# Neighbour sums on one core: 8 of 32 destination blocks from gathered rows, 24 dense, and X split by accumulating DMA

## The chip, the cores and the metric

The kernel runs on one core of one Trainium2 chip. Its time is the device time of one execution in microseconds; the kernel before takes 510.82 us as the median of 3 runs (510.23 to 510.98). TensorE (PE) multiplies matrices and loads weights (PEld), VectorE (DVE) and ScalarE (ACT) work along rows of 128 partitions, GpSimd (POOL) and SyncE (SP) mainly issue DMAs here. Each engine works through its own instructions in order and waits on semaphores of the others.

## The reference

```python
num_nodes, num_edges, dim = 4096, 65536, 128
output = np.zeros((num_nodes, dim), dtype=np.float32)
for i in range(len(edge_index_src)):
    output[edge_index_dst[i]] += node_features[edge_index_src[i]]
```

Source and destination indices are drawn at random, so that each of the 1024 pairs of a destination block and a source block (128 nodes each, 32 blocks) holds some 64 edges. Features are float32, and the sum must come out at float32 precision.

## The kernel before

The kernel turns the sum into dense matrix products. For a destination block d and a source block s, a 128 by 128 matrix A counts the edges from each source node to each destination node, and the output block is the sum over s of A transposed times the rows of X of block s. X is held as three bf16 parts whose sum is the float32 value (`x3`), so each product is made three times and summed in PSUM.

To build A, the edges have to be brought together by pair (d, s). The 65,536 edges lie as 128 partitions times 512, and are looked at as NCH = 24 chunks of up to NJ = 22 edges per partition. Two passes sort them:

- **Pass 1** (lines 105 to 195) sorts each chunk by destination block. A one-hot over the 32 blocks (`oh1`, line 128) is summed over the edges with a matmul against a triangle (`before`, line 131) and a chain of 21 adds (`cum1`, line 152), which gives each edge its rank in its block (`rank1`, lines 157 to 165). Then, for six quads of four chunks, a one-hot of the rank (`p1`, line 176 in the helper `onehot`) is multiplied against the keys (`v1`, line 141): 88 or 84 matmuls a quad (line 190). The results `sa` and `sbk` (lines 194 and 195) hold, for each chunk and block, up to 128 edges along the partitions.
- **The split of X** (lines 198 to 204) loads four quarters on the SP queue and makes the three bf16 parts by copies on ACT and subtractions on DVE in turn.
- **Pass 2** (`pass2`, lines 210 to 264) does the same again for a group of GD = 8 destination blocks, by source block: one-hots (line 215), counts (219), 23 adds (228), a product with the one-hot (229), ranks (232, 236), and for each destination block a one-hot of 24 by 128 (`p2`, line 176) and 24 matmuls (251). It is a generator; the main loop takes one step of it per slot.
- **The main loop** (lines 305 to 325) has a slot for each of the 32 destination blocks. `onehots` (line 276) builds two one-hots of 32 by 128 on DVE, `blocks` multiplies them into A for eight source blocks at a time (line 286, evicted by ACT at line 288), and `product` multiplies A of the slot before with `x3` (line 293: 96 matmuls of 128 by 128). `finish` copies the result on ACT (line 298) and stores it.

The order is written out by hand (`manual_schedule`): every engine runs its instructions in the order of the Python code. A pool with two buffers (`sb2`) lets DVE be up to two slots ahead of PE. `_general` is a slow path for inputs whose counts do not fit; it is behind a flag and does not run here.

Of the kernel before, what the change touches and what calls it, by code (L numbers as in the profile page):

```python
# [8 lines left out]
P = 128  # L9
# [7 lines left out]
NB = 32  # L17
NCH = 24
NJ = 22
NQ = NCH // 4  # L20
GD = 8
CODE0 = 0x2000


@with_exitstack
def kernel(
# [14 lines left out]

    nc = tc.nc
# [7 lines left out]
    flagp = ctx.enter_context(tc.tile_pool(name="flagp", bufs=1))  # L50
    fmax = flagp.tile([P, 8], F32, name="fmax")
    flag_i = flagp.tile([1, 1], I32, name="flag_i")

# [3 lines left out]
    with ExitStack() as fast:  # L57
        fast.enter_context(tc.manual_schedule())
        _fast(fast, tc, node_features, src32, dst32, out, cst, ident, fmax, flag_i, T)
# [6 lines left out]
def _fast(ctx, tc, X, src32, dst32, out, cst, ident, fmax, flag_i, T):  # L66
    nc = tc.nc
    V, S, G, PE = nc.vector, nc.scalar, nc.gpsimd, nc.tensor

    sb1 = ctx.enter_context(tc.tile_pool(name="sb1", bufs=1))  # L70
    sb2 = ctx.enter_context(tc.tile_pool(name="sb2", bufs=2))
    ps = ctx.enter_context(tc.tile_pool(name="ps", bufs=2, space=bass.MemoryType.PSUM))
# [3 lines left out]
    raw = sb1.tile([P, 7 * NT], I32, name="raw", tag="cum")  # L76
# [8 lines left out]
    V.memset(raws[:, T:, :], 0)  # L85

    identb = cst.tile([P, P], BF16, name="identb")
    V.tensor_copy(out=identb[:], in_=ident[:])

    before = cst.tile([P, P], BF16, name="before")  # L90
    G.memset(before[:], 1.0)
    G.affine_select(out=before[:], in_=before[:], pattern=[[1, P]], base=0,
                    channel_multiplier=-1, compare_op=OP.is_gt, fill=0.0)
    iota = cst.tile([P, P], U16, name="iota")
    G.iota(iota[:], pattern=[[1, P]], base=0, channel_multiplier=0)

    x3 = cst.tile([P, NB, 3, P], BF16, name="x3")
# [4 lines left out]
    kd = sb1.tile([P, NCH * NJ], BF16, name="kd")  # L102
# [3 lines left out]
    V.tensor_copy(out=kd[:], in_=blk_i)  # L106
# [5 lines left out]

    def by_quad(t):
        return t.rearrange("p (j q l) -> p q j l", q=NQ, l=4)

    S.activation(out=kb[:], in_=by_quad(sblk_i), func=mybir.ActivationFunctionType.Copy, bias=1.0)
    S.activation(out=ka[:], in_=by_quad(code_i), func=mybir.ActivationFunctionType.Copy,
                 bias=float(CODE0))
# [3 lines left out]

    JQ = NJ * NQ
    oh1 = sb1.tile([P, JQ, NB, 4], BF16, name="oh1", tag="oh")
    kdv = kd[:].rearrange("p (m l) -> p m l", l=4)
    psb = [ps.tile([P, 1024], F32, name=f"psb{h}", tag="psA") for h in range(2)]
    for b in range(NB):
        V.tensor_single_scalar(out=oh1[:, :, b, :], in_=kdv, scalar=float(b), op=OP.is_equal)
    for h in range(2):
        for j in range(NJ):  # L130
            PE.matmul(out=psb[h][:, :384], lhsT=before[:],  # L131
                      rhs=oh1[:, j * NQ:(j + 1) * NQ, 16 * h:16 * h + 16, :],
                      start=j == 0, stop=j == NJ - 1)
# [3 lines left out]
    def spread1(q):  # L137
        v1[q] = sb2.tile([P, NJ, 2, NB, 4], BF16, name="v1", tag="t1")
        ohq = oh1[:].rearrange("p (j q) b l -> p q j b l", q=NQ)[:, q]
        for k, key in ((0, kab), (1, kb[:])):  # L140
            V.tensor_tensor(out=v1[q][:, :, k], in0=ohq,  # L141
                            in1=key[:, q, :, None, :].to_broadcast([P, NJ, NB, 4]), op=OP.mult)

    spread1(0)
    cum1 = sb1.tile([P, NJ, NQ, NB, 4], BF16, name="cum1", tag="cum")
    oh1j = oh1[:].rearrange("p (j q) b l -> p j (q b l)", q=NQ)
    cum1j = cum1[:].rearrange("p j q b l -> p j (q b l)")
    for h in range(2):
        S.copy(out=cum1[:, 0, :, 16 * h:16 * h + 16, :],
               in_=psb[h][:, :384].rearrange("p (q b l) -> p q b l", q=NQ, b=16))  # L150
    for j in range(1, NJ):
        V.tensor_tensor(out=cum1j[:, j], in0=cum1j[:, j - 1], in1=oh1j[:, j - 1], op=OP.add)  # L152
    HJ = NJ // 2
    rank1 = sb1.tile([P, NQ, NJ, 4, 2], BF16, name="rank1")
    for h in range(2):
        js = slice(h * HJ, (h + 1) * HJ)
        V.tensor_tensor(out=cum1j[:, js], in0=cum1j[:, js], in1=oh1j[:, js], op=OP.mult)  # L157
        psr = ps.tile([P, 512], F32, name="psr", tag="misc")
        for b in range(NB):
            PE.matmul(out=psr[:, :HJ * NCH], lhsT=identb[:],  # L160
                      rhs=cum1[:, js, :, b, :].rearrange("p j q l -> p (j q) l"),
                      start=b == 0, stop=b == NB - 1)
        for k in range(2):
            S.copy(out=rank1[:, :, js, :, k],
                   in_=psr[:, :HJ * NCH].rearrange("p (j q l) -> p q j l", q=NQ, l=4))
    spread1(1)
    V.tensor_reduce(out=fmax[:, 0:1], in_=rank1[:].rearrange("p q j l k -> p (q j l k)"),
                    op=OP.max, axis=AX.X)


# [3 lines left out]
    def onehot(dst, keys2, n):  # L174

        V.tensor_tensor(  # L176
            out=dst.rearrange("p i (m k) -> p i m k", k=2),
            in0=iota[:, None, :].to_broadcast([P, n, P]).rearrange("p i (m k) -> p i m k", k=2),
            in1=keys2[:, :, None, :].to_broadcast([P, n, P // 2, 2]), op=OP.is_equal)

    for q in range(NQ):
        if q > 1:
            spread1(q)
        p1 = sb2.tile([P, NJ * 4, P], BF16, name="p1", tag="t2")
        onehot(p1[:], rank1[:, q].rearrange("p j l k -> p (j l) k"), NJ * 4)
        psm = ps.tile([P, 512], F32, name="psm", tag="misc")
        for l in range(4):
            js = [j for j in range(NJ) if j * NCH + q * 4 + l < T]
            for j in js:
                PE.matmul(out=psm[:, l * 64:(l + 1) * 64], lhsT=p1[:, j * 4 + l, :],  # L190
                          rhs=v1[q][:, j, :, :, l].rearrange("p k b -> p (k b)"),
                          start=j == js[0], stop=j == js[-1])
        pv = psm[:, :256].rearrange("p (l k b) -> p l k b", l=4, k=2)
        S.copy(out=sa[:, q * 4:q * 4 + 4, :], in_=pv[:, :, 0, :])
        S.copy(out=sbk[:, q * 4:q * 4 + 4, :], in_=pv[:, :, 1, :])


    for i in range(0, NB, 8):
        xf = sb2.tile([P, 8, P], F32, name="xf")
        nc.sync.dma_start(out=xf[:], in_=X[i * P:(i + 8) * P, :].rearrange("(s p) f -> p s f", p=P))  # L200
        for v in range(3):
            S.copy(out=x3[:, i:i + 8, v, :], in_=xf[:])  # L202
            if v < 2:
                V.tensor_tensor(out=xf[:], in0=xf[:], in1=x3[:, i:i + 8, v, :], op=OP.subtract)  # L204
# [3 lines left out]
    state = {}  # L208

    def pass2(g):  # L210
        d0 = g * GD
# [33 lines left out]
        for half in range(2):  # L245
# [9 lines left out]
            if half == 0:  # L255
                yield
# [166 lines left out]
```

## Time and profile before

| | |
|---|---|
| time, median of 3 runs | 510.82 us |
| the profiled execution's own time | 509.85 us |
| its span, first to last instruction | 507.9 us |
| mean granted TensorE clock | 0.818 |
| PE busy | 375.5 us (74%) |
| DVE busy | 366.0 us (72%) |
| ACT busy | 163.1 us (32%) |
| POOL busy | 1.5 us |
| DMA, all queues | 6.05 MB, mean 12 GB/s |

The span is the time from the first to the last instruction of the profiled execution; the execution took 1.95 us more than it, and the median of the runs is another 0.97 us longer. The busy shares of PE and DVE are near each other, but they are averages over stages in which now one and now the other is the bound, so the stages have to be read apart. The rows that the working rests on are quoted in the prediction. In them, L131 is line 131 of the kernel, "x44" a count of instructions, "busy, mean ns" the sum in us and the mean of one in ns, and what stands after the second bar is the idle time before them and what ended it.

### The profile page before, as it was taken

The page shows a single profiled execution, that of the slowest core. Times are in us where ns is not written, and L with a number is a line of the kernel's source. Part 1 is how long each engine was busy: PE and PEld are TensorE (multiplying, and loading weights), DVE is VectorE, ACT ScalarE, POOL GpSimd, SP SyncE. Part 2 cuts the span into 40 slices and gives each one's busy share as a digit, 9 for nine tenths or more (in the row PEclk, how much of TensorE's full clock was granted, in tenths as well). Part 3 has the DMA queues.
Part 4 walks back from the last instruction along what each step waited for, and adds up shares of the span by engine and source line. Part 5 has one row for each costly group of instructions (what it writes and reads, how often), then busy time and mean ns, then how long its engine had stood idle before and what let it go on. Part 6 is the DMA issues. An engine that isn't in the chain of part 4 may idle for free.

```text
span 507.9 us, 12335 instructions
## 1 busy us (share of the span) xinstructions
PE 375.5 (74%) x5709; PEld 358.5 (71%) x5709; DVE 366.0 (72%) x429; ACT 163.1 (32%) x213; POOL 1.5 (0%) x10
## 2 busy tenths in 40 slices
PE   0607574610339283999999499999949999999997
PEld 0305574610238283999999499999949999999996
DVE  5697999735859899566789956678995666655630
ACT  1001000045000050332656133265613326665652
POOL 1000000000000000000000000000000000000000
PEclk9957766665665596987999798799979879999999
DMA  5000000011000000000000000000000000000000
GB/s 165 1 0 1 1 1 0 1 43 41 0 0 1 2 1 5 8 6 3 12 14 8 5 8 6 3 12 13 8 5 8 7 2 13 13 9 12 12 13 14
DMA packets 9109, 6.05 MB, mean 12 GB/s; under 512 B 608, under 2 KB 8800, under 8 KB 9056
## 3 DMA queue, kind: packets, MB, share of 16 engines
q1 hardware_dynamic: 8912, 4.72, 3.3%
q8 instruction: 45, 0.74, 0.6%
q10 hardware_dynamic: 144, 0.52, 0.3%
q14 instruction: 8, 0.07, 0.0%
HBM read 3.15 MB, written 2.10 MB: 10 GB/s over the span
## 4 chain that ended last, share of the span: by engine, by line
PE 59%; DVE 31%; issue 5%; ACT 3%; DMA 1%; DVEq 0%; ACTq 0%
PE pso L293 32%; PE psa L286 11%; DVE p L176 9%; DVE cum L228 5%; PE ps L251 5%; PE psr L232 4%; DVE oh L276 4%; PE psb L219 3%; DVE cum L229 3%; DVE v L141 2%; DVE cum L152 2%; ACT x L202 2%; DVE xf L204 2%; PE psr L160 2%; PE psb L131 2%
## 5 line engine op out<-in xcount | busy, mean ns | idle before, releaser
L293 PE MATMUL pso<-x,a 128*128 128x128 bf16 x3072 | 200.2, 224 | 0.0
L293 PEld LDWEIGHTS <-a 128*128 128x128 bf16 x3072 | 185.3, 100 | 0.0
L288 ACT CAST a<-psa 128x1024 bf16<-128x1024 f32 x128 | 129.2, 1013 | 87.3 <-PE psa L286 87.0
L176 DVE TENSOR_TENSOR p<-iota,rank 128x3072 bf16<-128x3072 uint16 (+1 forms) x38 | 90.8, 2426 | 24.3 <-PE ps L251 24.3
L276 DVE TENSOR_TENSOR oh<-iotas,slo 128x4096 bf16<-128x4096 uint16 x32 | 73.2, 2289 | 45.1 <-PE psa L286 45.1
L286 PE MATMUL psa<-oh 128*128 128x128 bf16 x1024 | 81.8, 226 | 1.3 <-ACT a L288 1.3
L276 DVE TENSOR_TENSOR oh<-iota,dlo 128x4096 bf16<-128x4096 uint16 x32 | 73.1, 2284 | 0.0
L286 PEld LDWEIGHTS <-oh 128*128 128x128 bf16 x1024 | 65.9, 101 | 1.7 <-issue 1.6
L251 PE MATMUL ps<-ov,p 128*128 128x32 bf16 x768 | 50.2, 238 | 6.7 <-DVE p L176 6.0
L251 PEld LDWEIGHTS <-p 128*128 128x128 bf16 x768 | 46.1, 120 | 10.2 <-DVE p L176 10.2
L190 PE MATMUL psm<-v,p 128*128 128x64 bf16 x512 | 31.7, 239 | 23.6 <-DVE p L176 23.1
L190 PEld LDWEIGHTS <-p 128*128 128x128 bf16 x512 | 30.6, 123 | 24.7 <-DVE p L176 24.7
L232 PE MATMUL psr<-cum,identb 128*128 128x192 bf16 x128 | 20.2, 354 | 32.8 <-DVE cum L229 32.8
L232 PEld LDWEIGHTS <-identb 128*128 128x128 bf16 x128 | 18.3, 144 | 34.7 <-issue 21.8
L219 PE MATMUL psb<-ov,before 128*128 128x256 bf16 x96 | 14.5, 322 | 35.2 <-DVE ov L215 35.2
L219 PEld LDWEIGHTS <-before 128*128 128x128 bf16 x96 | 10.9, 115 | 38.2 <-issue 26.0
L228 DVE TENSOR_TENSOR cum<-cum,ov 128x256 bf16<-128x256 bf16 x92 | 26.8, 291 | 4.4 <-ACT cum L222 1.4
L160 PE MATMUL psr<-cum,identb 128*128 128x264 bf16 x64 | 9.7, 323 | 17.5 <-DVE cum L157 17.5
L204 DVE TENSOR_TENSOR xf<-xf,x 128x1024 f32<-128x1024 f32 x8 | 9.8, 1226 | 17.3 <-ACT x L202 17.3
L160 PEld LDWEIGHTS <-identb 128*128 128x128 bf16 x64 | 7.1, 112 | 20.2 <-DVE cum L157 17.9
L254 ACT CAST pa<-ps 128x128 bf16<-128x128 f32 x8 | 2.1, 266 | 53.2 <-PE ps L251 53.2
L236 ACT CAST rank<-psr 128x192 bf16<-128x192 f32 x8 | 2.5, 377 | 51.7 <-PE psr L232 51.7
(47 smaller groups left out, 146.7 us busy)
## 6 DMA issues: line engine op xcount, KB each, us to landing
xf<-in_node_features_dram SPq DMA_DIRECT2D x4, 512.0 KB, 5.1
out_dram<-res SPq DMA_DIRECT2D x32, 64.0 KB, 1.5
raw<-in_edge_index_src_dram ACTq DMA_DIRECT2D x1, 512.0 KB, 5.1
raw<-in_edge_index_dst_dram SPq DMA_DIRECT2D x1, 512.0 KB, 4.9
```

The source lines that it names most:

```text
L160: PE.matmul(out=psr[:, :HJ * NCH], lhsT=identb[:], rhs=cum1[:, js, :, b, :].rearrange("p j q l -> p (j q) l"), start=b == 0, stop=b == NB - 1)
L176: V.tensor_tensor(out=dst.rearrange("p i (m k) -> p i m k", k=2), in0=iota[:, None, :].to_broadcast([P, n, P]).rearrange("p i (m k) -> p i ...
L190: PE.matmul(out=psm[:, l * 64:(l + 1) * 64], lhsT=p1[:, j * 4 + l, :], rhs=v1[q][:, j, :, :, l].rearrange("p k b -> p (k b)"), start=j == ...
L204: V.tensor_tensor(out=xf[:], in0=xf[:], in1=x3[:, i:i + 8, v, :], op=OP.subtract)
L219: PE.matmul(out=psb2[:, :NB * GD], lhsT=before[:], rhs=oh2[:, c], start=c == 0, stop=c == NCH - 1)
L228: V.tensor_tensor(out=cum2[:, c], in0=cum2[:, c - 1], in1=oh2[:, c - 1], op=OP.add)
L232: PE.matmul(out=psr[:, :NCH * GD], lhsT=identb[:], rhs=cum2[:, :, s, :], start=s == 0, stop=s == NB - 1)
L251: PE.matmul(out=ps2[:, (d % 4) * NB:(d % 4 + 1) * NB], lhsT=p2[:, c, :], rhs=v2[:, c, :, d], start=c == 0, stop=c == NCH - 1)
L276: V.tensor_tensor(out=dst.rearrange("p i (m k) -> p i m k", k=2), in0=io[:, None, :].to_broadcast([P, NB, P]).rearrange("p i (m k) -> p i ...
L286: PE.matmul(out=psa[:, i * P:(i + 1) * P], lhsT=oh[0][:, s, :], rhs=oh[1][:, s, :], start=True, stop=True)
L288: S.copy(out=a[:, k * 8:k * 8 + 8, :], in_=psa[:].rearrange("p (s m) -> p s m", s=8))
L293: PE.matmul(out=pso[:, :P], lhsT=a[:, s, :], rhs=x3[:, s, v, :], start=s == 0 and v == 0, stop=s == NB - 1 and v == 2)
```

## The change

The change rewrites most of `_fast`. What is computed stays the same. In the order of the program:

- The four loads of X go to the start of the SP queue, behind the load of the destination indices. The split of X is now `x_part`: ACT writes minus the bf16 part, and a DMA on the POOL queue adds it to `xf` in place (`accum_op`), instead of a subtraction on DVE. There are two such rounds of four DMAs. After the third part, an SP DMA writes the three parts to a DRAM tensor `x3d`, one row of 768 bytes per node.
- Pass 1 is split into two halves of 12 chunks. The running counts of half 0 are adds on DVE as before, on half the width; those of half 1 are made by PE and ACT (`counts`: up to four matmuls of 128 by 384 and a copy for each of 22 steps), a pair of steps at a time between other work.
- The first KG = 8 destination blocks are not built densely. `gather_keys` makes a row index and a destination key for each slot of `sa`/`sbk` (8 small DVE instructions a quad). For each of the 48 pairs (block d, quad q), `gather` issues four indirect DMAs on the POOL queue, each fetching 128 rows of `x3d`, and `gather_sum` multiplies them with a one-hot of 4 by 128 (one DVE instruction, four matmuls of 128 by 384). Six buffers of the pool `xg`, the four of `xf` among them, let the gathers be six pairs ahead.
- Pass 2 and the main loop cover 24 blocks, in groups of 4, 6, 6 and 8. The chunks are ranked in two halves of 12, so that there are 11 adds of twice the width instead of 23, and `p2` is written as two one-hots of 12 by 64 into buffers whose other half was zeroed once.
- `product` is one matmul of 128 by 384 for a source block instead of three of 128 by 128, so the three parts stand side by side in PSUM. `finish` sums them with a reduction on DVE, and is called in the following slot, behind `onehots` and ahead of the step of pass 2.

The core of the diff:

```diff
+KG = 8
+GROUPS = (4, 6, 6, 8)
+GE = 2
...
+    NX = 4
+    BX = NB // NX
+    for i in range(NX):
+        xf.append(xg.tile([P, BX, P], F32, name="xf", tag="xg"))
+        nc.sync.dma_start(out=xf[i][:], in_=X[i * BX * P:(i + 1) * BX * P, :].rearrange(
+            "(s p) f -> p s f", p=P))
...
+    def x_part(i, v):
+        part = x3[:, i * BX:(i + 1) * BX, v, :]
+        S.activation(out=part, in_=xf[i][:], func=COPY, scale=-1.0)
+        if v < 2:
+            G.dma_start(out=xf[i][:], in_=part, accum_op=OP.add)
+        else:
+            nc.sync.dma_start(
+                out=x3d[i * BX * P:(i + 1) * BX * P, :].rearrange("(s p) w -> p s w", p=P),
+                in_=x3[:, i * BX:(i + 1) * BX, :, :].rearrange("p s v f -> p s (v f)"))
...
+    def counts():
+        c, o = flat(cum1[1]), flat(oh1[1])
+        for j in range(NJ):
...
+            todo = [(before, o[:, j])]
+            if j >= 1:
+                todo.append((ones, o[:, j - 1]))
+            if j >= 2:
+                todo += [(upto, o[:, j - 2]), (identb, c[:, j - 2])]
+            for i, (w, rhs) in enumerate(todo):
+                PE.matmul(out=to, lhsT=w[:], rhs=rhs, start=i == 0, stop=i == len(todo) - 1)
+            S.copy(out=c[:, j], in_=to)
...
+    def gather(d, q):
+        t = xg.tile([P, 4, 3 * P], BF16, name="rows", tag="xg")
+        for l in range(4):
+            G.indirect_dma_start(
+                out=t[:, l, :], out_offset=None, in_=x3d[:, :],
+                in_offset=bass.IndirectOffsetOnAxis(ap=gidx[:, place(q).start + l, d:d + 1], axis=0))
...
+    def gather_sum(d, q):
+        oh = sb2.tile([P, 4, P], BF16, name="ohg", bufs=6)
+        onehot(oh[:], gkey[:, place(q), d, :], 4)
...
+        for l in range(4):
+            PE.matmul(out=psg[d][:, :3 * P], lhsT=oh[:, l, :], rhs=t[:, l, :],
+                      start=q == 0 and l == 0, stop=q == NQ - 1 and l == 3)
...
+    def finish():
+        for d, pso in done:
+            res = sb2.tile([P, P], F32, name="res")
+            V.tensor_reduce(out=res[:], in_=pso[:, :3 * P].rearrange("p (v f) -> p f v", v=3),
+                            op=OP.add, axis=AX.X, negate=True)
+            nc.sync.dma_start(out=out[d * P:(d + 1) * P, :], in_=res[:])
...
+    count_on(3)
+    for i in range(NX):
+        x_part(i, 1)
+    count_on(1)
+    ranks(0)
+    for i in range(NX):
+        x_part(i, 2)
+    for q in range(NQ):
+        if q == QH:
+            ranks(1)
+        move1(q)
...
+        gather_keys(q)
+        ready = GE * (q + 1)
+        issue(min(summed + 6, ready))
+        if q >= 1:
+            add_up(GE * q)
...
     def product(k, a, pso):
         for s in range(k * 8, k * 8 + 8):
-            for v in range(3):
-                PE.matmul(out=pso[:, :P], lhsT=a[:, s, :], rhs=x3[:, s, v, :],
-                          start=s == 0 and v == 0, stop=s == NB - 1 and v == 2)
+            PE.matmul(out=pso[:, :3 * P], lhsT=a[:, s, :],
+                      rhs=x3[:, s, :, :].rearrange("p v f -> p (v f)"),
+                      start=s == 0, stop=s == NB - 1)
...
+    for g, gd in enumerate(GROUPS):
+        gen = pass2(g + 1) if g + 1 < len(GROUPS) else iter(())
+        step = 0
+        for i in range(gd):
+            oh = onehots(g, i)
+            finish()
+            while step < -(-STEPS * (i + 1) // gd):
+                next(gen, None)
+                step += 1
...
+            slot += 1
+            add_up(n0 + (len(order) - n0) * slot // slots)
```

What this does to the order on the engines shows at three places. **ACT, between pass 1 and the split of X.** Before, the twelve casts of the split (`x_91<-xf`) stand behind the last copies of pass 1 and ahead of the first ones of pass 2:

```order
L194 CAST sa<-psm 128x128
L195 CAST sbk<-psm 128x128
L202 CAST x_91<-xf 128x8x128 x12
L222 CAST cum_929<-psb_904 128x256
L236 CAST rank_989<-psr_956 128x192 x2
L254 CAST pa<-ps_996 128x128
```

In the change, on the same engine (`psc` are the counts of half 1, `rank_229` the ranks of half 0, `sa` the first quad's result):

```order
L207 CAST cum_204<-psc 128x384 x6
L165 ACTIVATE x_192<-xf 128x8x128 x4
L207 CAST cum_204<-psc 128x384 x2
L239 CAST rank_229<-psr 128x12x11 x2
L207 CAST cum_204<-psc 128x384 x2
L239 CAST rank_229<-psr 128x12x11 x2
L207 CAST cum_204<-psc 128x384 x2
L165 ACTIVATE x_192<-xf 128x8x128 x4
L207 CAST cum_204<-psc 128x384 x8
L273 CAST sa<-psm 128x128
```

The second and the third round of the split have moved ahead of copies that pass 1 needs, and each of their casts waits for an accumulating DMA of the round before it.

**POOL, the whole fast path behind its constants.** Before, nothing follows them. In the change (a piece of the difference):

```order
+L117 IOTA iota 128x128
+L118 IOTA iotas 128x128
+L122 MEMSET p2b_110 128x12x64
+L123 MEMSET p2b_110 128x12x64
+L122 MEMSET p2b_111 128x12x64
+L123 MEMSET p2b_111 128x12x64
+L167 DMA xf<-x_192 128x8x128 x8
+L303 DMA rows<-x3d,gidx 128x384 x192
```

The queue gets 8 accumulating DMAs and behind them 192 indirect ones.

**DVE, where a group's pass 2 begins in the main loop.** Before, in the first slots of the third group, with the first steps of the fourth group's pass 2 between them (`ov_4096` its one-hots and their products with the keys, `oh` the one-hots of a slot):

```order
L276 TENSOR_TENSOR oh<-iotas,slo_3160 128x4096
L276 TENSOR_TENSOR oh<-iota,dlo_3161 128x4096
L215 TENSOR_SCALAR ov_4096<-sbk 128x24x8 x32
L276 TENSOR_TENSOR oh<-iotas,slo_3160 128x4096
L276 TENSOR_TENSOR oh<-iota,dlo_3161 128x4096
L224 TENSOR_TENSOR ov_4096<-ov_4096,sa 128x6144
```

In the change, at the start of the second group (`pso` is a dense block's result, `psg` a gathered one's):

```order
L255 TENSOR_TENSOR oh<-iotas,slo_2092 128x4096
L255 TENSOR_TENSOR oh<-iota,dlo_2093 128x4096
L326 TENSOR_REDUCE res<-pso 128x128
L326 TENSOR_REDUCE res<-psg 128x128
L386 TENSOR_SCALAR oh_2190<-sbk 128x24x6 x32
L399 TENSOR_TENSOR v_2191<-oh_2190,sa 128x4608
L255 TENSOR_TENSOR ohg<-iota,gkey 128x512 x2
L255 TENSOR_TENSOR oh<-iotas,slo_2092 128x4096
L255 TENSOR_TENSOR oh<-iota,dlo_2093 128x4096
L326 TENSOR_REDUCE res<-pso 128x128
```

The reductions have come in between a slot's one-hots and the step of pass 2; each waits for PE to end the products of the slot before.

More of the change, by code (lines that the diff above doesn't have):

```diff
@@ L125, in _fast @@
[L125 to L128, printed above, removed]
[L129 to L133 removed]
+    x3 = sb1.tile([P, NB, 3, P], BF16, name="x3")
@@ L135, in _fast, with count_on @@
+    counting = counts()
+    def count_on(n):
+        for _ in range(n):
+            next(counting, None)
     v1 = {}
```

363 lines of the change are left out of this document (220 added, 143 removed).

## The prediction

> **What bounds the kernel now.** I cut the span into its stages first (busy time in windows; the columns are span, PE, PEld, DVE, ACT, POOL with their counts, granted clock, DMA share, GB/s):
>
> ```profile
> 0.00:50.30 50.30, 19.20 (x108) 12.04 (x108) 37.31 (x68) 4.98 (x9) 1.49 (x10) 0.83 0.14 42
> 50.30:104.00 53.70, 31.67 (x512) 30.63 (x512) 48.01 (x15) 2.57 (x13) 0.00 (x0) 0.68 0.01 1
> 104.00:125.30 21.30, 0.00 (x0) 0.00 (x0) 9.68 (x8) 11.13 (x12) 0.00 (x0) 0.52 0.17 49
> 125.30:167.40 42.10, 21.81 (x248) 18.85 (x248) 32.23 (x70) 2.56 (x6) 0.00 (x0) 0.58 0.00 1
> 256.10:344.90 88.80, 80.97 (x1276) 79.63 (x1274) 67.50 (x85) 35.94 (x46) 0.00 (x0) 0.88 0.03 8
> 433.70:507.90 74.20, 70.48 (x1262) 70.24 (x1259) 35.83 (x19) 39.75 (x48) 0.00 (x0) 1.00 0.04 12
> ```
>
> Pass 1 (to 104) is bound by DVE, the split of X (104 to 125.3) by ACT and DVE in turn with PE idle, the first pass 2 (to 167.4) mostly by DVE, and the main loop, 340.5 us, by PE: 8 slots with a pass 2 take 88.8 us, of which PE works 81. The chain in order of time shows the pace and the holes:
>
> ```profile
> 361.32 4.49 DVE oh L276 x2
> 373.21 3.37 DVE cum L229
> 376.62 5.06 PE psr L232 x32
> ...
> 393.78 1.59 PE ps L251 x24
> ...
> 434.84 1.34 PE pso L293 x24
> 436.63 1.34 PE pso L293 x24
> ...
> 497.38 6.70 PE pso L293 x120
> ```
>
> A quarter slot takes 436.63 - 434.84 = 1.79 us, so a slot 7.15; a matmul of 128 columns takes 6.70/120 = 56 ns. After a hole the clock is lower: 32 matmuls of 192 columns took 5.06 us, 158 ns each.
>
> **The change part by part.** It replaces nearly everything, so I build the new span from four stages. Durations come from these rows (mean ns behind the comma):
>
> ```profile
> 16.08 4.66 PEld L131 LDWEIGHTS <-before 128*128 128x128 bf16 x29 [0.17 <-issue]
> L128 DVE TENSOR_SCALAR oh<-kd 128x528 bf16<-128x528 bf16 x32 | 6.7, 305 | 0.0
> L215 DVE TENSOR_SCALAR ov<-sbk 128x192 bf16<-128x192 bf16 x128 | 15.5, 202 | 0.0
> L228 DVE TENSOR_TENSOR cum<-cum,ov 128x256 bf16<-128x256 bf16 x92 | 26.8, 291 | 4.4 <-ACT cum L222 1.4
> L152 DVE TENSOR_TENSOR cum<-cum,oh 128x768 bf16<-128x768 bf16 x21 | 11.7, 557 | 4.2 <-ACT cum L149 3.5
> L141 DVE TENSOR_TENSOR v<-oh,ka 128x2816 bf16<-128x2816 bf16 x6 | 9.7, 1618 | 0.1
> L224 DVE TENSOR_TENSOR ov<-ov,sa 128x6144 bf16<-128x6144 bf16 x4 | 13.4, 3351 | 0.0
> L239 DVE TENSOR_REDUCE fmax<-rank 128x1 f32<-128x384 bf16 x4 | 2.2, 553 | 9.9 <-ACT rank L236 9.9
> L332 DVE TENSOR_REDUCE fone<-psf 1x1 f32<-1x128 f32 x1 | 0.3, 280 | 16.5 <-PE psf L330 16.5
> L202 ACT CAST x<-xf 128x1024 bf16<-128x1024 f32 x12 | 12.3, 1044 | 10.3 <-DVE xf L204 10.3
> L288 ACT CAST a<-psa 128x1024 bf16<-128x1024 f32 x128 | 129.2, 1013 | 87.3 <-PE psa L286 87.0
> xf<-in_node_features_dram SPq DMA_DIRECT2D x4, 512.0 KB, 5.1
> out_dram<-res SPq DMA_DIRECT2D x32, 64.0 KB, 1.5
> q1 hardware_dynamic: 8912, 4.72, 3.3%
> 5.94 0.43 DVE L105 TENSOR_SCALAR raw<-raw 128x528 int32<-128x528 int32 x1 [4.03 <-DMA raw<-in_edge_index_dst_dram]
> 504.16 0.27 ACT L298 COPY res<-pso 128x128 f32<-128x128 f32 x1 [5.09 <-PE pso L293]
> ```
>
> From them: a matmul of 384 columns 4.66/29 = 0.161 us; a two-input DVE operation 0.16 us + 0.52 ns an element (291 at 256, 557 at 768, 1618 at 2816); a one-input bf16 comparison 0.07 us + 0.27 ns an element from start to start (0.21 at 528, 0.121 at 192).
>
> *Stage 1, to the keys of the first quad (R).* On DVE: start at 5.9, one-hots of half 0 in 32 x 0.14 = 4.4, with shifts 2.5, one-hots of half 1 4.4, first spread 3.1, 21 adds of 384 at 0.39 = 8.2, two products of 4224 at 2.3: 33.1. PE's sums and ACT's copies of the ranks add 3, and then PE has 88 matmuls of the quad (5.5) and 32 of the counts (5.2) with copies between: R is 49 at the earliest.
>
> The accumulating DMAs decide whether it stays there. They form a chain: the first cast ends near 8.6 (X behind the indices, one cast of 1.04), then eight DMAs on POOL in two rounds, then the last cast. ACT cannot copy the counts that PE waits for, nor `sa`, before those casts; PE then still has some 7.6 us of the quad. A DMA of that size (512 KB, 1024 rows) landed in 5.1 us from HBM. Queue 1 bounds it from below: 3.3% of 16 x 507.9 us over 8912 packets is 30 ns each, so 1024 on 16 engines cost 1.9 us; from above I take twice 5.1, because an accumulate reads and writes its target. No accumulate is in the trace. I take 5.1, the row of the same size: 8.6 + 8 x 5.1 + 1.0 + 7.6 = **R 58**; by the bounds 49 (the floor) and 99. The 9.7 us of subtractions and the whole stage 104 to 125.3 go in exchange.
>
> *Stage 2, five more quads.* DVE per quad: four one-hots of 2816 at 1.54, a spread 3.1, eight small key operations near 0.15 each, two gather one-hots 0.8: 11.3. Five are 56.5; the ranks of half 1 add 7.7 (two products 4.7, wait 3), the ends 0.2: **64.4**. POOL has 8 indirect DMAs a quad, so they are covered up to 1.4 us each.
>
> *Stage 3, the first pass 2*, with 4 blocks instead of 8: one-hots 3.0, PE's counts and copy 2.9, 11 adds 3.5, product 1.8, PE's ranks and copies 3.0, first `p2` 1.0, then PE, 4 x 24 matmuls at 1.6 (the 1.59 row) = 6.4, copy and keys 1.0, two results 1.2: **23.8**, where before it took 42.
>
> *Stage 4, the main loop*, bound by PE:
> - Blocks and products: 32 x 56 ns + 32 x 0.1625 = 6.99 a slot against 7.15, so the wide product wins little; the 24 slots instead of 32 are what counts. With the first slot's blocks at ACT's pace (4 x 1.01): 170.2.
> - 35 of the 48 gathered pairs, four matmuls of 0.1625 each: 22.8.
> - Three pass 2: counts 10.6 (half of them at the low clock), ranks 6.6, 20 x 1.6 for `ps2`: 49.2.
> - Waits. `finish` stands ahead of the step of pass 2, so DVE starts on that step only when PE has ended the products before; what PE needs of it, PE waits for. The one-hots of pass 2 are covered by nothing in slots 4 and 10 (4.1 and 3.9 plus 2 at a low clock) and 0, where the slot's own one-hots are added (7.9); the first `p2` of each group costs 1.7 to 2.4; a late one-hot 1.0 and 1.7: 27.0. Queued behind a waiting `finish` are the step, the gather one-hots and the next slot's one-hots, 4.49. Without a step these are 0.6 + 0.6 + 4.5 = 5.7, under PE's 7.9, so the last 8 slots stay with PE. The reduction is not in the trace; L239 gives 0.55 for 384 bf16, L332 0.28 for 128 from PSUM: I take 0.6, and bound it by 0.28 and 1.1 (twice).
> - The end: the last reduction and store, 4.2 (before, 504.2 to 507.9 and the copy).
>
> Sum **273.4**, against 340.5.
>
> *The gathers.* 192 indirect DMAs in a row on POOL; `add_up` makes PE wait for them, and with PE everything behind. None is in the trace. The nearest row is the 64 KB store of 128 rows, 1.5 us to landing; 128 packets of 30 ns on 16 engines would be 0.3; the other end is the 5.1 of the 1024 rows. I take 1.5, and that is covered: 59 + 192 x 1.5 = 347, while PE asks for the last one near 405. Uncovered it starts to cost at (405 - 59)/192 = 1.8.
>
> One rule speaks against this. The longest DVE instruction is 2.29 us (4.49 for two). The Trainium skill, "SBUF — State Buffer", section "Who interferes with whom", says that a DVE instruction with two SBUF inputs contends with a GpSimd instruction that reads SBUF, and that one in a two-port mode shuts GpSimd out until it ends. By it, each indirect DMA, whose indices lie in SBUF, could wait for a running one-hot; the time would then be that of rival 2 or 3. No run here shows it, since POOL is busy for 1.5 us in all.
>
> Span: 58 + 64.4 + 23.8 + 273.4 = 419.6. The profiled execution took 1.95 more than its span, the median 0.97 more than that: **423**.
>
> **The rivals.**
> 1. *The accumulating DMAs are slow*: a cast, a read and a write per element, 1024 short rows each. For it: R hangs on eight of them in a chain. Against: POOL and the DMA queues are empty there. Each us more in one adds 8 from 3.8 on; at 10.2, R is 99 and the time 464. DVE's comparisons (7 to 17 us) holding the first round until 17 would add 8: 431, inside the forecast.
> 2. *POOL sets the pace*: at 2.0 us a gather, the last lands at 59 + 384 = 443, then a sum, the last products and the end, 10: 456 with the 3 outside the span.
> 3. *Slower than before*: the same queue at a price that eats everything. 59 + 192c + 13 = 511 gives c = 2.3. Where each indirect DMA waits out a one-hot of 2.29, the time is 512, and with 0.4 of its own, 589. For it: DVE is busy most of each slot. Against: many DVE operations are shorter (0.3 to 0.6), and any gap serves.
> 4. *DVE becomes the bound of every slot*: were the reduction or the small operations 2.2 us longer in a slot than I have them, `finish` would tie DVE and PE into one chain; 24 slots at 2 us more are 48: 471.
> 5. *No gain*: the narrow one-hots and fewer blocks saving only what the gathers add, 511; the 57 us of eight slots speak against it.
>
> **How the numbers follow.** The forecast, 405 to 446, has 0.60; rival 1 0.17; rival 2 0.10; rival 3 0.07; rival 4 0.05; rival 5 0.01. The low end is R at its floor (414) less 3% for durations read from other shapes, 402; the high end takes in rivals 1, 2 and 4, 472. Outside stay rival 3 and the tails of the others, under 0.2. Faster by over 0.2% (about what a measurement of this kernel can tell from no change): 0.92; within 0.2%: 0.01; slower: 0.07.
>
> **What would show it.** Right: ACT's first `sa` copy near 57 behind casts that wait for `xf`; the first slot near 146; slots of 7.9 us at the end with PE never waiting for `rows`; POOL's queue done before 350. Wrong: PE's sums of gathered rows waiting for DMAs slot after slot (rivals 2 and 3), a first round of accumulates past 40 us (rival 1), or `psa` waiting for `oh` in the last eight slots (rival 4).

## The result and the profile after

The change takes 431.98 us, the median of 4 runs (430.21 to 433.11), against 510.52 us before (508.3 to 510.98): a ratio of 0.847, with a 95% interval of 0.843 to 0.850. The forecast was 423, in a range from 402 to 472. The profiled execution has a span of 430.3 us, at a mean granted clock of 0.852. One thing has to be said at once: in a later session the same program took 474.5 us, beside a kernel before that took 510.8 as ever. The experiments below are of four later sessions, each on another chip (0, 10, 2 and 5 on record; that of the result is not noted), and most of what they taught came from this difference.

The busy times by stage in the result's trace, cut at the prediction's places (columns as there: span, PE, PEld, DVE, ACT, POOL, clock, DMA share, GB/s):

```profile
0.00:61.50 61.50, 33.53 (x249) 21.37 (x249) 38.76 (x105) 25.38 (x42) 20.00 (x23) 0.89 0.82 171
61.50:127.80 66.30, 44.90 (x530) 35.72 (x531) 59.87 (x91) 4.29 (x17) 49.36 (x39) 0.69 0.24 57
127.80:156.70 28.90, 14.50 (x170) 10.45 (x169) 16.37 (x62) 1.11 (x5) 23.41 (x19) 0.57 0.26 63
156.70:207.90 51.20, 41.28 (x446) 32.09 (x445) 44.17 (x78) 17.13 (x21) 43.28 (x27) 0.81 0.23 55
207.90:275.80 67.90, 61.79 (x618) 45.37 (x617) 52.92 (x89) 25.24 (x29) 56.63 (x38) 0.92 0.26 63
275.80:349.80 74.00, 67.53 (x670) 50.56 (x669) 57.38 (x92) 26.04 (x30) 62.11 (x39) 0.93 0.24 58
349.80:420.00 70.20, 70.19 (x600) 47.73 (x598) 41.52 (x38) 32.38 (x32) 49.93 (x35) 1.00 0.26 63
420.00:430.30 10.30, 0.27 (x1) 0.08 (x1) 1.21 (x5) 0.00 (x0) 0.00 (x0) 0.60 0.04 10
```

The first four stages of the forecast stand in these rows:

| stage | forecast, us | measured, us |
|---|---|---|
| 1, to the first keys | 58 (floor 49) | 61.5 |
| 2, five quads | 64.4 | 66.3 |
| 3, first pass 2 | 23.8 | 28.9 |
| 4, main loop to PE's last product | 269.2 | 263.3 |
| the end | 4.2 | 10.3 |
| span | 419.6 | 430.3 |

PE works 240.8 us of the loop's 263.3 (the sum of the four rows from 156.70 on), so 22.5 are waits; forecast were 242.2 and 27.0. The column of POOL is the surprise: it is busy for 43 of 51, 57 of 68, 62 of 74 us. The page's group of the gathers:

```profile
L303 POOL DMA_INDIRECT rows<-x3d,gidx x192 | 284.7, 1483 | 90.1 <-issue 57.5
```

From the timeline (start, duration, engine), a gather beside the compares of pass 2, and the last gather:

```profile
209.04 3.50 DVE L386 TENSOR_SCALAR oh<-sbk 128x144 bf16<-128x144 bf16 x32
209.12 3.55 POOL L303 DMA_INDIRECT rows<-x3d,gidx  x1 [0.30 <-issue]
...
409.15 0.95 POOL L303 DMA_INDIRECT rows<-x3d,gidx  x1 [0.30 <-issue]
```

The mean of 1483 ns is close to the 1.5 us of the forecast, but 0.30 us lie between two gathers even when nothing is waited for. From the first at 62.66 to the last at 409.15 it is 346.5/191 = 1.81 us from start to start. The forecast had 347 us for the end of the queue and 1.8 as the price from which it costs.

### The profile page after: what moved, and what is told of

Same layout as the page of the kernel before. It is cut to its first block, busy times and chain, and to the rows that moved or that the text cites. A ratio compares the mean times of both kernels' runs of the same rounds, so it can differ in the third digit from the quotient of the medians.

```text
span 430.3 us, 7817 instructions
## 1 busy us (share of the span) xinstructions
PE 334.0 (78%) x3274; PEld 243.4 (57%) x3274; DVE 312.2 (73%) x556; ACT 131.6 (31%) x174; POOL 304.7 (71%) x215
## 4 chain that ended last, share of the span: by engine, by line
PE 59%; DVE 28%; issue 3%; DMA 3%; ACT 3%; POOL 2%; DVEq 0%
PE pso L462 26%; PE psa L456 9%; PE ps L425 7%; PE psg L318 6%; DVE oh L255 5%; DVE p L255 4%; PE psc L206 3%; PE psm L268 3%; DVE cum L405 3%; DVE v L223 3%; DVE oh L143 3%; DVE oh L386 3%; PE psr L235 2%; DMA rows<-x3d,gidx 2%; PE psb L393 2%
## 5 line engine op out<-in xcount | busy, mean ns | idle before, releaser
L303 POOL DMA_INDIRECT rows<-x3d,gidx x192 | 284.7, 1483 | 90.1 <-issue 57.5
L462 PE MATMUL pso<-x,a 128*128 128x384 bf16 x768 | 144.2, 333 | 0.0
L458 ACT CAST a<-psa 128x1024 bf16<-128x1024 f32 x96 | 96.8, 1013 | 117.5 <-PE psa L456 117.5
L462 PEld LDWEIGHTS <-a 128*128 128x128 bf16 x768 | 72.8, 100 | 40.2 <-issue 3.8
L318 PE MATMUL psg<-rows,ohg 128*128 128x384 bf16 x192 | 44.8, 370 | 28.4 <-DVE ohg L255 15.1
L255 DVE TENSOR_TENSOR p<-iota,rank 128x2816 bf16<-128x2816 uint16 x24 | 37.4, 1619 | 9.8 <-ACT rank L239 9.8
L268 PEld LDWEIGHTS <-p 128*128 128x128 bf16 x512 | 31.4, 120 | 10.5 <-DVE p L255 8.7
L425 PE MATMUL ps<-v,p2b 128*128 128x32 bf16 x576 | 29.3, 224 | 5.6 <-DVE p2b L255 5.6
L425 PEld LDWEIGHTS <-p2b 128*128 128x128 bf16 x576 | 28.4, 119 | 6.8 <-DVE p2b L255 5.3
L255 DVE TENSOR_TENSOR p2b<-iota,rank 128x768 bf16<-128x768 uint16 x48 | 23.6, 555 | 11.9 <-ACT rank L416 11.0
L167 POOL DMA_DIRECT2D xf<-x x8 | 15.6, 2912 | 14.5 <-ACT x L165 14.5
```

Of the source, the lines that this page charges most:

```text
L167: G.dma_start(out=xf[i][:], in_=part, accum_op=OP.add)
L255: V.tensor_tensor(out=dst.rearrange("p i (m k) -> p i m k", k=2), in0=io.rearrange("p i (m k) -> p i m k", k=2), in1=keys2[:, :, None, :]. ...
L268: PE.matmul(out=psm[:, l * 64:(l + 1) * 64], lhsT=p1[:, l % 2, j, :], rhs=v1[q][:, j, :, :, l].rearrange("p k b -> p (k b)"), start=j == j ...
L303: G.indirect_dma_start(out=t[:, l, :], out_offset=None, in_=x3d[:, :], in_offset=bass.IndirectOffsetOnAxis(ap=gidx[:, place(q).start + l, ...
L318: PE.matmul(out=psg[d][:, :3 * P], lhsT=oh[:, l, :], rhs=t[:, l, :], start=q == 0 and l == 0, stop=q == NQ - 1 and l == 3)
L425: PE.matmul(out=ps2[:, d * NB:(d + 1) * NB], lhsT=p2[:, c, :], rhs=v2[:, c, :, d], start=c == 0, stop=c == NCH - 1)
```

## The experiments

**What the gathers buy.** All 32 blocks dense:

```diff
-KG = 8
-GROUPS = (4, 6, 6, 8)
+KG = 0
+GROUPS = (4, 6, 6, 8, 8)
```

> Edit of the change: no gathered blocks at all; all 32 destination blocks are dense, in groups of 4, 6, 6, 8 and 8, without the keys, the gathers and the copy of X to DRAM, everything else as in the change. Theory (the gathers buy eight slots of 7 us and one pass 2, and pay for them with their own matmuls and DVE work): 432 + 8 x 7.0 + 21 of pass 2 - 48 x 0.65 of gathered products - 12 of gathered one-hots and keys - 12 to 14 of waits for rows and the longer end: about 452, range 445 to 465, the end after the last DVE operation falling from 8.6 to about 3 us. Rival (the gathers are most of the gain, the rest of the change is worth 20 us or less): 490 or more.

Measured: 472.51 us, ratio 0.924 (0.922 to 0.926). It lies between the two theories; my sum of 452 was 20 too low. Against the result's 432, which is of an earlier session, the gathers are worth some 40 us and the rest of the change some 38. After the last DVE operation (469.1) the span goes on for 3.4 us, as before the change (3.2) and not for 8.6 as in the change (421.7 to 430.3). This kernel still has the eight accumulating DMAs, so the 5 us at the end come with the gathers or with the copy of X that they read; what they are spent on no row shows.

**The reductions behind the step, and more gathers.** In the first, `finish()` moves behind the step of pass 2; in the second, POOL gets 24 gathers more, which nobody reads:

```diff
             oh = onehots(g, i)
-            finish()
             while step < -(-STEPS * (i + 1) // gd):
                 next(gen, None)
                 step += 1
+            finish()
```

> Edit of the change: the reductions and stores of the slot before are called behind the slot's step of pass 2 instead of ahead of it. Theory A (PE and DVE bound the loop, and the 27 us of waits put down to the reductions ahead of the step are real): PE's waits for DVE's oh and p2b (14.9 + 4.5 us in the loop) mostly go, and the time falls by 8 to 12 us, to 420 to 424. Theory B (the queue of 192 gathers on POOL, 1.78 us apiece from start to start and never idle, paces the loop): PE only comes earlier to rows that have not landed; PE's waits for DMA rows grow from 0 in the loop, and the time falls by 0 to 5 us, to 427 or more.

```diff
+        if (d * NQ + q) % 2 == 0:
+            u = sb2.tile([P, 3 * P], BF16, name="extra", bufs=2)
+            G.indirect_dma_start(out=u[:], ...)
```

> Edit of the change: with every second gathered pair one more indirect DMA is issued, into a buffer that nobody reads (216 instead of 192 on POOL). Theory B (POOL is full from 63 to 410 us): 24 more at 1.5 to 1.8 us each push the last rows back by 36 to 43 us, of which a few us are slack: 462 to 472. Theory of the prediction (the queue is covered and has room until 350): below 435, no change beyond 3 us.

Measured: 472.0 and 499.2 us. No theory had the first: neither a gain of 8 nor one of 0 to 5, but 40 us more than the result. Nor did one have the second, which lies 27 us above the 472 at the upper end of theory B. The first kernel's trace has stretches in which PE waits with no cause that the profile can name, the first of them ahead of the first moved instruction. So the change itself had to run again.

**The change, unaltered.**

> The change, unaltered, on the chip of these runs, since the kernel with the reductions behind the step took 472 and lost some 35 us in stretches in which PE, DVE and ACT wait for signals that the profile cannot name, some of them before the first instruction that the edit moves. Theory D (such a stretch comes when POOL issues gathers back to back, 1.25 us apart, for more than some ten of them; the order of the change happens to break those runs up): 430 to 434 again, at most a few us of waits without a name. Theory E (the lost time belongs to this chip or to the hour, not to the edit): 460 or more.

Measured: 474.5 us (472.35 to 476.95). By its number theory E held: the lost 43 us belong to the session, or to its chip, and not to any edit. The same cut of its trace, at the same instructions:

```profile
0.00:60.85 60.85, 35.48 (x249) 22.04 (x249) 38.72 (x104) 25.36 (x42) 19.79 (x23) 0.86 0.82 173
60.85:131.47 70.62, 45.24 (x529) 36.11 (x530) 59.78 (x90) 4.32 (x17) 50.53 (x40) 0.70 0.21 55
131.47:180.90 49.43, 17.57 (x170) 11.74 (x169) 17.00 (x62) 1.11 (x5) 33.28 (x33) 0.57 0.27 66
180.90:464.78 283.88, 246.32 (x2329) 178.00 (x2327) 197.32 (x302) 100.31 (x111) 184.73 (x120) 0.89 0.20 50
```

Stage 3 takes 49.4 us where it took 28.9, with 33 gathers in it instead of 19. There its timeline reads:

```profile
158.56 0.95 POOL L303 DMA_INDIRECT rows<-x3d,gidx  x1 [0.30 <-issue]
159.00 0.19 PE L425 MATMUL ps<-v,p2b 128*128 128x32 bf16 x1 [0.46 <-issue]
...
159.70 0.26 PE L425 MATMUL ps<-v,p2b 128*128 128x32 bf16 x3 [0.52 <-issue]
159.81 0.95 POOL L303 DMA_INDIRECT rows<-x3d,gidx  x1 [0.30 <-issue]
161.06 0.94 POOL L303 DMA_INDIRECT rows<-x3d,gidx  x1 [0.30 <-issue]
...
161.80 0.26 PE L425 MATMUL ps<-v,p2b 128*128 128x32 bf16 x3 [1.83 <-issue]
...
161.84 0.56 DVE L255 TENSOR_TENSOR p2b<-iota,rank 128x768 bf16<-128x768 uint16 x1 [4.41 <-remote]
```

PE gets a few matmuls through every 0.7 us or a multiple of it, where the result's trace has 96 of them in 3.8 us. DVE waits for a signal whose sender the profile cannot find ("remote"), and POOL issues gathers 1.25 us apart all the while.

The first time that something is late comes much earlier, at ACT's second copy of `sa`. PE's matmuls for it and the copy, first in the result's timelines, then in those of the change run again:

```profile
69.16 4.15 PE L268 MATMUL psm<-v,p 128*128 128x64 bf16 x66
73.34 0.27 ACT L273 CAST sa<-psm 128x128 bf16<-128x128 f32 x1 [3.46 <-PE psm L268]
...
68.53 4.14 PE L268 MATMUL psm<-v,p 128*128 128x64 bf16 x66
74.01 0.27 ACT L273 CAST sa<-psm 128x128 bf16<-128x128 f32 x1 [4.78 <-PE psm L268]
```

The copy starts 0.03 us after PE's last matmul in the one and 1.34 us after it in the other. Up to there POOL has started eight gathers in both, counted from its first one at the same times within 0.01 us. So the order and the spacing of the gathers do not tell the two apart; what does is not known.

**Do the gathers do that?** Two measurements by themselves. The first shows what sets the length of a gather, the second what a run of gathers does to PE and ACT.

> A measurement by itself: the whole computation is left out (the output is a copy of the features). Five times 24 indirect DMAs of 128 rows of 768 bytes are issued on POOL while DVE is idle, runs uint16 one-hots of 128x4096 with two inputs, runs bf16 compares of 192 elements with one input, runs bf16 compares of 4096 elements, and runs reductions of 4096. Theory (the DVE operation that runs beside it sets how long POOL takes to issue a gather): 0.95 us with DVE idle, 1.9 to 2.5 beside the one-hots, 3 to 4 beside either compare, 0.95 to 1.2 beside the reductions. Rival (it is the DMA queue or PE's and ACT's traffic that lengthens them): about 1.0 to 1.2 in all five phases.

The five stretches, in that order (columns: span, DVE, POOL, clock, DMA share, GB/s):

```profile
23.00:54.00 31.00, 0.00 (x0) 22.84 (x24) 1.00 0.46 133
56.00:112.50 56.50, 55.68 (x25) 49.12 (x24) 1.00 0.14 40
116.00:146.20 30.20, 21.73 (x83) 22.70 (x24) 1.00 0.26 75
237.00:295.00 58.00, 56.45 (x48) 51.08 (x23) 1.00 0.13 37
295.00:326.50 31.50, 31.50 (x8) 23.64 (x25) 1.00 0.27 78
```

A gather takes 0.95 us beside an idle DVE, 2.02 beside the two-input one-hots (with the 0.30 between them one gather in each one-hot of 2.29), 2.22 beside long compares and 0.95 beside reductions. Two stretches missed the 3 to 4 us of the theory: the 2.22 beside long compares, and 0.95 beside short ones. The short ones stand 30.2/83 = 0.36 us apart, with gaps; the 32 of the change, 109 ns each without a gap, hold a gather for 3.55. DVE decides the length; the rival fell. The Trainium skill, "SBUF — State Buffer", section "Who interferes with whom", has a DVE instruction with two SBUF inputs contend with a GpSimd one that reads SBUF, and a reduction never contend; the trace agrees, with 2.02 and 0.95.

> A measurement by itself; the whole computation is left out (the output is a copy of the features). Four times a chain of 40 links PE to ACT to PE, and behind it a stream of 96 weight loads and matmuls of 32 columns without a wait: with POOL idle, beside 44 indirect gathers back to back, beside 44 gathers with a 512-element memset between each two, and beside 44 gathers while DVE runs uint16 one-hots of 128x4096. Theory D (a run of gathers 1.25 us apart holds up signals and PE's issue): links of 0.6 to 0.8 us with POOL idle, several times that in the second phase, the first length again in the third and the fourth. Rival (gathers do not touch the signals; the unnamed waits have another source): the same length of link and the same stream, within 10%, in all four.

```profile
11.60:36.00 24.40, 11.19 (x136) 6.76 (x135) 0.56 (x4) 8.69 (x41) 0.13 (x1) 1.00 0.63 191
36.00:100.10 64.10, 13.82 (x136) 7.96 (x136) 0.01 (x1) 8.51 (x40) 41.87 (x44) 1.00 0.26 77
100.10:125.00 24.90, 11.39 (x136) 6.86 (x136) 0.59 (x5) 8.69 (x41) 21.59 (x29) 1.00 0.20 56
175.60:200.00 24.40, 11.34 (x136) 6.86 (x136) 24.06 (x12) 8.69 (x41) 21.18 (x11) 1.00 0.13 37
```

In each row PE does the same 40 links and 96 matmuls (columns as in the rows by stage of the result). The stretch takes 24.4 us with POOL idle, 24.9 with a memset between the gathers, 24.4 beside one-hots, and 64.1 beside gathers back to back. In the second stretch, from the timelines of POOL and PE:

```profile
51.72 0.94 POOL L106 DMA_INDIRECT t<-xd,idx  x1 [0.30 <-issue]
...
52.97 0.21 PE L112 MATMUL psl<-link,unit 128*128 128x64 bf16 x1 [0.30 <-issue]
...
53.98 0.21 PE L112 MATMUL psl<-link,unit 128*128 128x64 bf16 x1 [0.80 <-ACT link L113]
...
55.38 0.21 PE L112 MATMUL psl<-link,unit 128*128 128x64 bf16 x1 [1.19 <-issue]
...
57.48 0.21 PE L112 MATMUL psl<-link,unit 128*128 128x64 bf16 x1 [1.89 <-issue]
...
88.70 0.19 PE L115 MATMUL pss<-link,unit 128*128 128x32 bf16 x1 [2.61 <-issue]
...
90.55 0.94 POOL L106 DMA_INDIRECT t<-xd,idx  x1 [0.30 <-issue]
...
91.50 0.18 PE L115 MATMUL pss<-link,unit 128*128 128x32 bf16 x1 [2.61 <-issue]
...
98.50 1.52 PE L115 MATMUL pss<-link,unit 128*128 128x32 bf16 x50 [0.49 <-issue]
```

For the first 13 gathers a link takes 0.51 us as with POOL idle (0.6 to 0.8 were expected). Then it takes 1.4 or 2.1, and the stream, in which nothing waits for another engine, gets one matmul out every 2.8 us. Some 7 us after the last gather PE runs freely again. So in this measurement the gathers held PE up, and it took a run of some 13. That is shown; through what they do it is not.

That it is their spacing is not shown. In the third stretch PE was done after 15 gathers and in the fourth after 11, and the third does not end clean: ACT copies the result of the stream 1.27 us after PE's last matmul (124.52 to 125.79), against 0.09 with POOL idle. A longer run 1.66 us apart may hold PE up as well. One more rival is untested: every time on record comes with a span and a clock from the profiler, so what is held up may be its recording and not the program by itself.

**Stage 1.** The casts of the split apart, and the subtraction back on DVE:

```diff
-    count_on(3)
     for i in range(NX):
+        count_on(1)
         x_part(i, 1)
-    count_on(1)
     ranks(0)
-    for i in range(NX):
-        x_part(i, 2)
...
             count_on(1)
+            if q == 0:
+                x_part(l, 2)
```

> Edit of the change: the second and third round of casts of X stand one by one between the copies of the counts instead of four in a row. Theory (the bursts of four casts, 3.9 us each, hold up the copies of the counts and PE with them): the first keys come at 55 to 58 us instead of 61.5, and the rest of the program follows, 3 to 6 us less than the change. Rival (the accumulating DMAs set the pace of stage 1): the first keys within 1 us of 61.5 or later. The time of the whole run can hide either, so the first keys decide.

```diff
-            G.dma_start(out=xf[i][:], in_=part, accum_op=OP.add)
+            V.tensor_tensor(out=xf[i][:], in0=xf[i][:], in1=part, op=OP.add)
```

> Edit of the change: the subtractions of the split are on DVE again (8 of them, 128x1024) instead of accumulating DMAs on POOL. Theory (the DMAs take 9.8 us off DVE, and cost it 2.2 us by slower compares in the one-hots of half 1): the one-hots of half 1 fall from 6.7 to 4.5 us, the subtractions add 8 x 1.2, and the first keys come at 66 to 70 us instead of 61.5. Rival (the DMAs are what holds stage 1 back): first keys at 58 or earlier.

The first keys came at 59.63 and at 67.44, against 60.85 in the same session. The casts in a row cost 1.2 us, not 3 to 6; the last cast now comes later, so the first gather waits for the copy of X until 64.2, and the whole run takes 480.0. The second came as expected. The two halves of the one-hots in the timeline of the result:

```profile
7.31 4.50 DVE L143 TENSOR_SCALAR oh<-kd 128x264 bf16<-128x264 bf16 x32
...
13.77 6.70 DVE L143 TENSOR_SCALAR oh<-kd 128x264 bf16<-128x264 bf16 x32
```

and in that of the kernel with the subtraction on DVE:

```profile
7.21 4.50 DVE L143 TENSOR_SCALAR oh<-kd 128x264 bf16<-128x264 bf16 x32
...
13.05 4.50 DVE L143 TENSOR_SCALAR oh<-kd 128x264 bf16<-128x264 bf16 x32
```

POOL's accumulating DMAs cost DVE 2.2 us while it runs the second half, and yet the first keys come 6.6 us earlier with them. The whole run took 484.9, with the stretches without a name in it as in all the runs of that session.

**Fewer gathers, spaced gathers.** Six gathered blocks, then a memset behind each gather, then the reductions behind the step, with the memset and without it:

```diff
-KG = 8
-GROUPS = (4, 6, 6, 8)
-GE = 2
+KG = 6
+GROUPS = (4, 6, 8, 8)
+GE = 1
...
+            G.memset(fill[:], 0.0)
```

> Edit of the change: 6 gathered blocks instead of 8, one of them instead of two during pass 1, and 26 dense blocks in groups of 4, 6, 8 and 8: 144 gathers, so that POOL has room. It is the base of the next two. Theory D (gathers 1.25 us apart for more than some ten hold up signals and PE): POOL fills its 24 buffers ahead in long runs whenever DVE is idle, so the stretches without a name remain: 445 to 470, with over 8% of the chain on issue and on an unknown queue. Rival (only a full POOL, 192 gathers, brings them): 425 to 440 and under 5%.

> Edit of the kernel with 6 gathered blocks: a memset of 512 elements on POOL behind every gather, so that no two are less than 1.66 us apart. Nothing else. Theory D: the stretches without a name go (under 5% of the chain), and the time falls by 10 us or more under the same kernel without the memsets, to 430 to 445, although POOL has 100 us more to do. Rival (the spacing does not matter): the memsets cost what they take where PE waits for rows, and the time is the same or 5 to 20 us longer.

> Edit of the spaced kernel with 6 gathered blocks: the reductions and stores behind the step of pass 2, as tried before, now without the stretches that hid it. Theory (27 us of waits in the loop come from the reductions ahead of the step): 6 to 12 us less than the spaced kernel. Rival (PE waits for the step anyway): within 3 us of it.

> Edit of the kernel with 6 gathered blocks, without the memsets: the reductions and stores behind the step of pass 2. In the kernels so far the stretches without a name stand only where twelve or more gathers follow each other with starts no more than 1.6 us apart; the kernel with 6 gathered blocks has no run of nine. Theory (the reductions ahead of the step cost 8.7 us, as in the spaced pair, and no run of twelve comes up): 435 to 439, with no run of twelve gathers and under 5% of the chain on issue. Rival (the earlier step lets POOL run ahead in long runs again): 445 or more, and a run of twelve or more in the trace.

Measured, in this order: 445.5, 455.15, 446.4 and 460.0 us. For the first, the time lies at the lower edge of theory D, and the 4% of the chain without a name with the rival. The memsets had nothing to mend, since the base had no stretch without a name, and cost 9.7: as a test of the spacing inside the kernel this pair failed. The reductions behind the step gave 8.7 in the spaced pair, as expected. Without the memsets the kernel with the edit took 14.5 us more, but in the next session and on another chip. By time and trace this is what the rival said, with a run of 19 gathers from 140.2 on and PE again let through in steps of 0.7 us (its timeline):

```profile
149.08 0.23 PE L425 MATMUL ps<-v,p2b 128*128 128x32 bf16 x2 [1.65 <-issue]
...
149.19 0.95 POOL L303 DMA_INDIRECT rows<-x3d,gidx  x1 [0.30 <-issue]
...
150.44 0.95 POOL L303 DMA_INDIRECT rows<-x3d,gidx  x1 [0.30 <-issue]
150.51 0.19 PE L425 MATMUL ps<-v,p2b 128*128 128x32 bf16 x1 [1.20 <-issue]
```

The rival's reason did not hold: this run, too, stands ahead of the first moved instruction. From the first slot's one-hots to the last DVE operation the kernel with the edit is faster, 280.7 us against 287.1. And here, too, the gathers do not tell the two kernels apart where it begins: from 133 to 143 us POOL starts them in the same steps in both, yet ACT copies the ranks 2.94 us after PE's last matmul for them with the edit (141.94 to 144.88) and 0.04 without it (141.52 to 141.56).

The change and its variants, but for the one with 24 gathers more, with POOL's longest run of gathers (starts at most 1.6 us apart, counted in its rows) and the share of the chain of waits that is "issue" or "another core or an unknown queue":

| kernel | chip | longest run | share | us |
|---|---|---|---|---|
| the change, in the result | not noted | 10 | 3% | 432.0 |
| the change, again | 10 | 21 | 16% | 474.5 |
| reductions behind the step | 0 | 20 | 18% | 472.0 |
| casts apart | 10 | 20 | 21% | 480.0 |
| subtraction on DVE | 10 | 21 | 15% | 484.9 |
| 32 dense blocks | 0 | none | 3% | 472.5 |
| 6 gathered | 2 | 8 | 4% | 445.5 |
| 6, spaced | 2 | 1 | 4% | 455.2 |
| 6, spaced, behind the step | 2 | 1 | 5% | 446.4 |
| 6, behind the step | 5 | 19 | 8% | 460.0 |

Every trace with a run of nineteen or more has the stretches, none with a run of up to ten has them. But that does not show that the run comes first. In the change run again PE starts to go in steps of 0.7 us at 153.99, when five gathers of the run of 21 had started. And the sessions divide the table just as well: all kernels with gathers on chips 0, 10 and 5 have the stretches, none on chip 2 or in the result has them. What the table does show is that they come with gathers: in one session on chip 0, the kernel without them has no stretch. With six blocks they came too, on chip 5. Whether six instead of eight make them rarer stays open, since the two were never run in one session. No version beat the result's 432; where the run comes up, the gathers of the change buy nothing over 32 dense blocks (474.5 and 472.5).

## Why the prediction was right, and where it was not

The direction, the size and the main loop were right by their own reasons. A quarter slot at the end takes 1.74 us (two products of the result's trace), 6.96 a slot where 6.99 was worked out:

```profile
390.86 1.46 PE L462 MATMUL pso<-x,a 128*128 128x384 bf16 x8
...
392.60 1.46 PE L462 MATMUL pso<-x,a 128*128 128x384 bf16 x8
```

In the last 70.20 us PE works 70.19, so DVE's reductions bind nothing there, as the step on `finish` said; they take 557 ns against 0.6. Moving them behind the step takes 4.6 to 9.8 us off the loop (the three pairs with and without the edit, of which only the spaced one, with 9.8, is of one session), so the waits that they cause are a part of the 22.5, not all of them. Of the signs named for being right, the slots of 7.9 us at the end came (two from 381.68 to 397.60, 7.96 each); the first slot came at 156.7 instead of 146.

**The step on the gathers failed.** "I take 1.5, and that is covered": the price left out the 0.30 between two gathers and what DVE does to them, and POOL's queue ended at 410, not before 350. That the time still came out is luck by a hair: PE's waits for rows (us in total, times, longest; from the view of waits) all lie in stage 3,

```profile
PE psg L318 <- DMA rows<-x3d,gidx: 11.8, 9, 3.5
```

and none in the loop. The kernel with 24 gathers more took 24.7 us more than the unaltered change run again; a covered queue would have swallowed them, but the two are of different sessions, and the stretches without a name may have had a part in it. The rule that was weighed against the change held: gathers do wait out one-hots. But DVE leaves POOL enough idle time (in the loop it works 196 of 263 us) that the mean is 1.81 and not the 2.3 of rival 3. Nor is 2.29 us the longest DVE instruction, as was said there: the prediction's own row of L224 has 3.35, and the longest gather of the result takes 4.90.

**Stage 1 came near for a wrong reason.** The chain of eight accumulating DMAs at 5.1 us did not decide it. They land in 8.2 us, but the four of a round overlap, and ACT found them done and ran its casts in one go (a row of the page's DMA issues, and ACT's timeline):

```profile
xf<-x POOLq DMA_DIRECT2D x8, 512.0 KB, 8.2
```

```profile
27.66 3.90 ACT L165 ACTIVATE x<-xf 128x1024 bf16<-128x1024 f32 x4
...
44.77 3.90 ACT L165 ACTIVATE x<-xf 128x1024 bf16<-128x1024 f32 x4
```

What was off was the floor of 49, by 12.5. Its terms add up to 46.8 (33.1, 3, 5.5 and 5.2), so 2.2 were left for the copies between PE's counts, and they were not worked out. The casts in a row are 1.2 of that, and the slower one-hots 2.2 if all of it reaches the keys. PE's waits for the count copies, 10.9 us in all, may hold most of the rest, but that is argued: with the casts apart these waits fell to 7.1, and the keys came only 1.2 earlier. The chain of DMAs would have decided from 4.0 us apiece on (17.2 + 8 x 4.0 = 49), not from 3.8; that slip changes nothing.

Stage 3 is 5.1 longer since PE waits there for rows: the queue that was to be covered was late by then, held by compares (a gather of 3.82 us at 127.19). The end was mis-sized by 6.1, and its cause stays open.

No rival had what happened in the later sessions; in the one in which the change ran again its time, 474.5, lies outside the stated range. Rival 2, POOL as the pace, comes nearest in the time (456), but there PE would wait for rows, and in the unaltered change run again it waits for them less than in the result. Two things stay open: what a run of gathers holds up, and why one and the same program is held up in one session and not in another. That the state keeps itself up, since a DVE that is held up no longer slows POOL, fits the traces (the 13 gathers from 158.56 to 173.55 of the change run again take 0.95 each) but was only argued.

## What to carry to other kernels

Price an indirect DMA by POOL's time from start to start, beside the DVE work that will run with it (here 1.25 us alone, 2.3 beside one-hots, nearly 4 beside back-to-back compares), and compare the whole queue with the time at which its last row is asked for. Be wary of a dozen and more of them back to back next to engines that depend on each other, and look for waits without a name in the chain. Fewer gathers ahead, or other work between them, may help; no run here shows that either does. Run a kernel that leans on such a queue more than once, in more than one session, before its time is believed.

## What the runs showed of the hardware that was not expected

- In one session, on chip 10, a run of indirect gathers 1.25 us apart slowed PE's issue after some 13 of them, from 96 matmuls in 2.7 us to one every 2.8 us, and a link from PE to ACT and back from 0.51 to 1.4 or 2.1 us. In the two sessions of the change, the same eight gathers at the same times went with a copy on ACT that came 1.3 us late in the one and in time in the other.
- A gather's length follows DVE: 0.95 us alone and beside reductions, 2.02 beside two-input one-hots, 2.22 beside compares of 4096 elements, 3.55 beside 32 short compares without a gap, and 0.95 beside short compares 0.36 us apart. The one-hots themselves stay at 2.29.
- The contention goes the other way with accumulating DMAs: 32 compares of DVE took 6.7 us instead of 4.5.
- With gathers the execution ends 8.6 to 11.4 us after its last DVE operation, without them 3.2 to 3.4.
